# A decoder layer with two attention groups on one core: index evacuation, load order, projection order, last feed-forward block and closing work rearranged

## The chip, the cores and the metric

The kernel runs on one core of one Trainium2 chip. Its engines are TensorE (matrix products into PSUM), VectorE (DVE in the rows), ScalarE (ACT), GpSimd (POOL), and SyncE (SP), whose queue issues nearly all transfers. The metric is the device time of one execution in microseconds (us). All times of the rows are us from the first instruction of the program, unless marked ns.

## The reference, cut to what matters

One layer on 256 tokens of width 1024, all in 32-bit floats:

```python
a = rmsnorm(h, g_attn)
qa, ka, va, qi, ki, wi, qb, kb, vb = split(a @ w_in)   # rope on qa, ka, qi, ki, qb, kb; layernorm on ki first
score = sum_h w_h * relu(qi_h . ki)                     # token index: the top 64 earlier keys of each query
y_a = softmax(qa . ka over those keys) @ va             # 8 heads share one key/value head
y_b = softmax(qb . kb, causal) @ vb                     # 8 heads; one block of 256 keys here
h = h + concat(y_a, y_b) @ w_out
f = rmsnorm(h, g_ffn)
h = h + (silu(f @ w_gate) * (f @ w_up)) @ w_down        # inner width 2816
u = rmsnorm(h, g_ple)
h = h + sigmoid(u @ w_ple_gate) * (p @ w_ple_proj)
return rmsnorm(h, g_final)
```

## The kernel before, in words

**Products.** Every large product is made of three matmuls per tile, `mm3` (L169): each operand x is held as a rounded part H and a remainder L = x - H, and H.H, H.L and L.H are added up in PSUM. Activations are the stationary operand (128 by 128), weights the moving one (up to 512 columns). There are two token tiles, t = 0 and 1.

**Weights.** They come in chunks of mostly 1 MB in the order of `CHUNKS` (L40 to L52), one DMA each on SP's queue. `load` (L99) issues the DMA and has ScalarE round the chunk to `hi` in pieces of 1024 columns (L127); `split` (L131) has VectorE subtract to get `lo` (L154). `need` (L163) loads three chunks ahead and splits the one asked for. Most chunks rotate through three buffers each of `raw`, `hi` and `lo`, so a chunk's `hi` and `lo` can be written once TensorE is done with the chunk three before.

**Order.** TensorE's order is the order in which the code issues (L74). That of VectorE, ScalarE, GpSimd and SP is made by a scheduler, which takes the ready instruction of highest priority; priority is the order of issue, raised by `urgent`. Its order is fixed before the run and follows its own idea of times. From L774 on, the orders of TensorE, ScalarE and VectorE are those of the code.

**Start.** 36 small matmuls on zeros (`warm`, L206) run while the first data come. `load_a` (L212) brings x transposed and the first group of `w_in` columns, slice by slice. After these and the chunks of group 1, SP issues x by rows (`h`, L246), the table of cosines and sines (L248) and the gain of the index key (L250), and then `load(NS + 5)` the next three chunks (L257). ScalarE sums the squares of `h` (L256).

**Projections.** `piece` and `group` (L295, L311) multiply column group by column group: group 0 holds ka, va, qi, ki and wi, group 1 qb, 2 kb, 3 vb, 4 qa. The group's 8 slices run as 8 steps of six matmuls; after each, `tick` calls what the plan (L508 to L537) hangs there: transposes (`tp_idx`, `tp_rope`, `tp`), products of queries and keys (`qk_idx`, `qk`), products with the values (`pv`) and the top-64 search (`topk`). `evac_g0` (L333) takes group 0 out of PSUM: layernorm statistics, the norm of x by Newton steps on VectorE (`rsqrt`, L180), tables scaled by it for keys (`kcs`, VectorE) and queries (`qcs`, GpSimd, L349), then va, the index weights and the rotated index queries and keys (`r0`). `evac_rope` (L378) does the rotation of a later group.

**Attention.** Units B (all earlier keys) and A (selected keys) come as B[0], B[1], B[2], A[0], A[1], A[2]: the first of each is token tile 0 with all heads, the others tile 1 with four heads each. `qk` ends with the softmax: VectorE adds the mask and finds the least value (L454), ScalarE takes exponentials (L460), VectorE scales (L466). A's mask is `dmask`, which `topk` makes (L419). Ticks `pp` lie in the product p @ w_ple_proj, `wb` in the rows of w_out that belong to B (kk = 4 to 7), `wa` in those of A (kk = 0 to 3, tile 0).

**Feed-forward.** Six blocks of the inner width, five of 512 columns and one of 256. Each multiplies by w_gate for both tiles (j = 0), then by w_up (j = 1); `hid_T` (L662) transposes the product of a finished tile. Then come w_down (L710 on) and the gated embedding (`ple_mms`, `ple_evac`, L730 on).

**Close.** `ple_evac` (L740) applies the sigmoid, adds to `h`, sums squares (on ScalarE where no sum comes before it, otherwise on VectorE) and has GpSimd multiply by the last gain. Tile 1's second half runs as two blocks of 256 columns (L779). The two copies that scale tile 0 for the output (L785) are issued after the first of these. After the second come a square root (L788), a reciprocal and the last scaling: half the columns on VectorE with the gain (L791), half on ScalarE (L793), with one DMA each.

Of the kernel before, what the change touches and what calls it, by code (L numbers as in the profile page):

```python
# [16 lines left out]
P = 128  # L17
D = 1024
# [10 lines left out]
LOOK = 3  # L29
WARM = 36  # L30
NS = 2
# [8 lines left out]
def _chunks():  # L40

    out = []
    order = [(1, k, 1) for k in range(NS)] + [(1, k, 2) for k in range(NS, KD, 2)]
    order += [(g, k, 4) for g in range(2, 5) for k in (0, 4)]
    out += [(f"g{g}", k, nk, IN_GROUPS[g][1] - IN_GROUPS[g][0], "w_in", IN_GROUPS[g][0]) for g, k, nk in order]
    out.append(("pp", 0, 2, D, "w_ple_proj", 0))
    out += [("wo", k0, 2, D, "w_out", 0) for k0 in (4, 6, 0, 2)]
    for b, (f0, fw) in enumerate(FF_BLOCKS):
        out += [(f"f{b}_{j}", k0, 4, fw, w, f0) for j, w in enumerate(("w_gate", "w_up")) for k0 in (0, 4)]
# [9 lines left out]
def layer_kernel(  # L59
# [117 lines left out]
    def tsl(t):  # L177
        return slice(t * P, (t + 1) * P)
# [86 lines left out]
    with actx:  # L265
# [29 lines left out]
        def piece(g, pss, k, ts):  # L295

            if g == 0:
                (wH, wL), r = g0[k], slice(None)
            else:
                c0 = max(c[1] for c in chunks if c[0] == f"g{g}" and c[1] <= k)  # L300
                wH, wL = need(f"g{g}", c0)
                wH, wL = wH[:, k - c0, :], wL[:, k - c0, :]
            width = wH.shape[1]
            for n, (aT, wT) in enumerate(((XH, wH), (XL, wH), (XH, wL)) if len(ts) > 1 else ((XH, wH), (XH, wL), (XL, wH))):
# [68 lines left out]
        def tp_idx(t):  # L373
            transpose4(r0s[t].rearrange("p h d -> p (h d)"), idxT, t, f"tidx{t}")
# [127 lines left out]
        def at_tick(key, *fs):  # L502
            plan.setdefault(key, []).extend(fs)
# [169 lines left out]
    for b, (f0, w) in enumerate(FF_BLOCKS):  # L673
        pgu = {}
        for j in range(2):
            for t in range(NT):
                ps = acc(f"ff{b}{t}{j}")
                for k in range(KD):
                    wH, wL = need(f"f{b}_{j}", k - k % 4)
                    mm3(  # L680
                        ps[:, :w], FH[:, k, tsl(t)], FL[:, k, tsl(t)], wH[:, k % 4, :], wL[:, k % 4, :],
                        k == 0, k == KD - 1,
                    )
                    if (b, j, t) == (0, 0, 0) and k in (4, 7):
                        trn(1, int(k == 7), FH, FL, "f")
                pgu[(j, t)] = ps
                if b == 0 and (j, t) == (0, 0):
                    rf[1] = rstd_h(1, "f")
                if pend:
                    hid_T(*pend.pop(0))  # L690
                if j == 0:
                    sg = ff.tile([P, NQ], F32, tag="sg", name=f"sg{b}{t}", bufs=3)
                    nc.scalar.activation(sg[:, :w], ps[:, :w], AF.Silu, scale=rf[t])  # L693
                    pgu[("s", t)] = sg
                else:
                    hid = ff.tile([P, NQ], F32, tag="hid", name=f"hid{b}{t}", bufs=3)
                    nc.vector.scalar_tensor_tensor(  # L697
                        hid[:, :w], ps[:, :w], rf[t], pgu[("s", t)][:, :w], op0=ALU.mult, op1=ALU.mult
                    )
                    pend.append((b, t, hid, w))  # L700
# [8 lines left out]

    for k in range(TAILK):  # L710
# [28 lines left out]

    def ple_evac(t, f0, w, ps, prev):  # L740
        cc = slice(f0, f0 + w)
# [5 lines left out]
        s3 = sm.tile([P, 1], F32, tag="s3", name=f"s3{t}{f0}")  # L747
        if prev is None:
            nc.scalar.activation(sqt[:, :w], h[:, t, cc], AF.Square, accum_out=s3)
        else:  # L750
            nc.vector.tensor_tensor_reduce(
                sqt[:, :w], h[:, t, cc], h[:, t, cc], 1.0, prev, ALU.mult, ALU.add, s3
            )
# [20 lines left out]
    with tc.manual_schedule(engines={mybir.EngineType.PE, mybir.EngineType.Activation, mybir.EngineType.DVE}):  # L774
        sp = ple_evac(1, 0, NQ, ps, None)
        m = sm.tile([P, 1], F32, tag="m3", name="m30")
        nc.vector.tensor_scalar(m, s0, 1.0 / D, EPS, op0=ALU.mult, op1=ALU.add)
        r = rsqrt(m, 1, "o0")
        for j in range(2):  # L779
            ps = acc(f"pg11{j}")  # L780
            ple_mms(1, 1, ps, j * 256, 256)
            sp = ple_evac(1, NQ + j * 256, 256, ps, sp)
            if j == 0:
                for a in (0, NQ):
                    nc.scalar.activation(h[:, 0, a : a + NQ], h[:, 0, a : a + NQ], AF.Copy, scale=r)  # L785
                    nc.sync.dma_start(out[tsl(0), a : a + NQ], h[:, 0, a : a + NQ])
        rt = sm.tile([P, 1], F32, tag="m3", name="rt")
        nc.scalar.activation(rt, sp, AF.Sqrt, bias=eps, scale=1.0 / D)  # L788
        r = sm.tile([P, 1], F32, tag="m3r", name="r1")
        nc.vector.reciprocal(r, rt)  # L790
        nc.vector.scalar_tensor_tensor(h[:, 1, NQ:], h[:, 1, NQ:], r, gB["fin"][:, NQ:], op0=ALU.mult, op1=ALU.mult)  # L791
        nc.sync.dma_start(out[tsl(1), NQ:], h[:, 1, NQ:])
        nc.scalar.activation(h[:, 1, :NQ], h[:, 1, :NQ], AF.Copy, scale=r)  # L793
        nc.scalar.dma_start(out[tsl(1), :NQ], h[:, 1, :NQ])

# [15 lines left out]
def _pack(inputs):  # L811
# [4 lines left out]
    def rows(w):  # L816
# [42 lines left out]
```

## Time and profile before

| | |
|---|---|
| median of 3 runs | 339.21 us (339.17 to 339.3) |
| the profiled execution | 339.18 us |
| its span, first to last instruction | 337.4 us |
| granted TensorE clock, mean | 0.996 |
| TensorE busy | 326.0 us, 97% of the span |
| VectorE busy | 226.1 us, 67% |
| ScalarE busy | 175.4 us, 52% |
| moved by DMA | 59.71 MB, mean 177 GB/s |

A timeline row gives start, duration, engine, line, operation, output and inputs, shapes, the count of instructions merged into it, and in brackets the idle time of the engine before it and who ended it. Matmuls overlap in the rows (a row's duration is longer than the distance to the next start), so a matmul's cost is the distance of starts. PEld is the load of the stationary operand, which overlaps the matmul before it.

### The profile page before, as it was taken

How to read it: one execution, taken by the hardware profiler on the slowest of the kernel's cores; microseconds unless marked ns; L12 is line 12 of the kernel's file. 1: busy time of each engine (PE TensorE's matmuls, PEld its weight loads, DVE VectorE, ACT ScalarE, POOL GpSimd, SP SyncE). 2: the span in 40 equal slices, each digit the busy share in tenths (PEclk: the TensorE clock that was granted, in tenths of full speed). 3: DMA queues.
4: the chain of work that ended last, by engine and by line, in shares of the span. 5: the costliest groups of instructions: out<-in, count | busy, mean ns of one | idle time of the engine just before them, and what ended most of it. 6: DMA issues, size and time to landing. Idle time of an engine off the chain costs nothing.

```text
span 337.4 us, 4461 instructions
## 1 busy us (share of the span) xinstructions
PE 326.0 (97%) x1688; PEld 268.2 (79%) x1688; DVE 226.1 (67%) x459; ACT 175.4 (52%) x280; POOL 6.9 (2%) x17
## 2 busy tenths in 40 slices
PE   8999899998999999999999999999999999999991
PEld 8886777776777888888888888889988888888890
DVE  3969999999996695535644655344673535379854
ACT  4865366667785475533553454324643424238524
POOL 2000000000000000000000000000000000000130
PEclk9999999999999999999999999999999999999998
DMA  7995694301933056356436634344785555550003
GB/s 263 421 375 216 243 349 152 125 2 34 339 111 110 32 200 246 130 236 246 142 120 243 248 105 150 121 124 158 287 300 184 193 172 202 176 199 1 2 0 124
DMA packets 10677, 59.71 MB, mean 177 GB/s; under 512 B 1312, under 2 KB 1440, under 8 KB 4640
## 3 DMA queue, kind: packets, MB, share of 16 engines
q1 hardware_dynamic: 10512, 59.17, 48.8%
q8 instruction: 13, 0.21, 0.2%
q10 hardware_dynamic: 144, 0.26, 0.2%
q14 instruction: 8, 0.07, 0.1%
HBM read 58.38 MB, written 1.05 MB: 176 GB/s over the span
## 4 chain that ended last, share of the span: by engine, by line
PE 83%; DVE 10%; ACT 4%; issue 1%; ACTq 0%; DVEq 0%
PE ff L172 12%; PE ff L170 12%; PE ff L171 12%; PE g L306 9%; PE wd L171 6%; PE wd L170 6%; PE wd L172 6%; PE wo L170 2%; PE wo L172 2%; PE wo L171 2%; DVE lo L154 2%; PE pg L172 2%; PE pg L170 2%; PE pg L171 2%; PE hidt L666 1%; PE warm L206 1%
## 5 line engine op out<-in xcount | busy, mean ns | idle before, releaser
L154 DVE TENSOR_TENSOR lo<-raw,hi 128x1024 fp32r<-128x1024 f32 (+1 forms) x99 | 116.8, 1209 | 61.5 <-ACT hi L127 61.5
L127 ACT CAST hi<-raw 128x1024 fp32r<-128x1024 f32 (+1 forms) x99 | 99.0, 1040 | 95.8 <-PE ff L172 44.6
L170 PE MATMUL ff<-hi,FH 128*128 128x512 f32 (+1 forms) x192 | 72.4, 377 | 0.0
L172 PE MATMUL ff<-hi,FL 128*128 128x512 f32 (+1 forms) x192 | 71.4, 372 | 0.0
L171 PE MATMUL ff<-lo,FH 128*128 128x512 f32 (+1 forms) x192 | 71.3, 371 | 0.0
L172 PEld LDWEIGHTS ff<-hi,FL 128*128 128x128 f32 x192 | 36.1, 188 | 6.3
L171 PEld LDWEIGHTS ff<-lo,FH 128*128 128x128 f32 x192 | 36.2, 189 | 6.0
L170 PEld LDWEIGHTS ff<-hi,FH 128*128 128x128 f32 x192 | 36.2, 188 | 5.9
L170 PE MATMUL wd<-hi,hidH 128*128 128x512 f32 x88 | 35.1, 399 | 0.0
L171 PE MATMUL wd<-lo,hidH 128*128 128x512 f32 x88 | 35.0, 397 | 0.0
L172 PE MATMUL wd<-hi,hidL 128*128 128x512 f32 x88 | 34.5, 393 | 0.0
L306 PE MATMUL g<-hi,XH 128*128 128x512 f32 x64 | 25.9, 410 | 0.0
L306 PE MATMUL g<-hi,XL 128*128 128x512 f32 x64 | 24.9, 393 | 0.0
L306 PE MATMUL g<-lo,XH 128*128 128x512 f32 x56 | 21.8, 395 | 1.8 <-DVE lo L154 1.8
L170 PEld LDWEIGHTS wd<-hi,hidH 128*128 128x128 f32 x88 | 16.5, 188 | 4.0
L172 PEld LDWEIGHTS wd<-hi,hidL 128*128 128x128 f32 x88 | 16.5, 188 | 4.0
L171 PEld LDWEIGHTS wd<-lo,hidH 128*128 128x128 f32 x88 | 16.5, 188 | 3.7
L670 DVE TENSOR_TENSOR hidL<-hidt,hidH 128x512 fp32r<-128x512 f32 (+1 forms) x12 | 7.7, 644 | 12.8 <-ACT hidH L669 12.8
L697 DVE SCALAR_TENSOR_TENSOR hid<-ff,f_y,sg 128x512 f32<-128x512 f32 (+1 forms) x12 | 8.4, 704 | 11.5 <-PE ff L172 11.5
L693 ACT ACTIVATE sg<-ff,f_y 128x512 f32<-128x512 f32 (+1 forms) x12 | 7.8, 647 | 15.6 <-PE ff L172 15.6
L306 PEld LDWEIGHTS g<-hi,XH 128*128 128x128 f32 x64 | 12.1, 189 | 3.4 <-issue 1.0
L306 PEld LDWEIGHTS g<-lo,XH 128*128 128x128 f32 x56 | 10.5, 188 | 4.5 <-DVE lo L154 2.7
(199 smaller groups left out, 457.6 us busy)
## 6 DMA issues: line engine op xcount, KB each, us to landing
raw<-in_w_dram SPq DMA_DIRECT2D x46, 1024.0 KB, 4.9
a<-in_xa_dram SPq DMA_DIRECT2D x8, 354.5 KB, 6.7
raw<-in_w_dram SPq DMA_DIRECT2D x5, 512.0 KB, 3.6
raw_g<-in_w_dram SPq DMA_DIRECT2D x2, 512.0 KB, 8.0
h<-in_x_dram SPq DMA_DIRECT2D x1, 1024.0 KB, 9.9
out_dram<-h SPq DMA_DIRECT2D x3, 256.0 KB, 2.1
raw<-in_w_dram SPq DMA_DIRECT2D x2, 256.0 KB, 4.5
gBffn<-in_g_ffn_dram SPq DMA_DIRECT2D x1, 512.0 KB, 6.5
```

Of the source, the lines that this page charges most:

```text
L127: nc.scalar.copy(hi[:, o : o + step], raw[:, o : o + step])
L154: nc.vector.tensor_tensor(lo[:, o:e], raw[:, o:e], hi[:, o:e].bitcast(F32), op=ALU.subtract)
L170: nc.tensor.matmul(ps, aH, wH, start=start, stop=False)
L171: nc.tensor.matmul(ps, aH, wL, start=False, stop=False)
L172: nc.tensor.matmul(ps, aL, wH, start=False, stop=stop)
L206: nc.tensor.matmul(wps[:, :P], wz, wz, start=i == 0, stop=i == WARM - 1)
L306: nc.tensor.matmul(pss[t][:, :width], aT[:, k, tsl(t)], wT, start=k == 0 and n == 0, stop=k == KD - 1 and n == 2,)
L666: nc.tensor.transpose(pt[:, i * P : (i + 1) * P], hid[:, i * P : (i + 1) * P], ident)
L670: nc.vector.tensor_tensor(hidL[:, kk, tsl(t)], pv, hidH[:, kk, tsl(t)].bitcast(F32), op=ALU.subtract)
L693: nc.scalar.activation(sg[:, :w], ps[:, :w], AF.Silu, scale=rf[t])
L697: nc.vector.scalar_tensor_tensor(hid[:, :w], ps[:, :w], rf[t], pgu[("s", t)][:, :w], op0=ALU.mult, op1=ALU.mult)
```

## The change

- 33 matmuls in `warm` in place of 36; at slice 0 of groups 0 and 1 the product with the weights' remainder runs ahead of that with x's remainder.
- The chunk for slices 0 to 3 of group 2 is loaded ahead of `h`, the table and the index gain.
- `evac_g0` is cut in two: `norm_g0` (statistics, norms, `kcs`, `qcs`) stays; what takes va, the index weights and the rotated index queries and keys out of PSUM comes after group 1, its rotation and one more split of weights. `tp_idx` moves from ticks g3 0 and 1 to g3 4 and 5, `qk_idx` from g3 4 and 5 to g3 7 and g4 0; kb's transposes go to g4 0 and 1, B[0].qk to g4 2, B[1].pv to pp 3, B[2].pv to wb 1, and A[0].qk runs ahead of the last transpose of qa.
- The projection with w_out runs all four kk of tile 0 and then those of tile 1.
- The last feed-forward block has w_gate's and w_up's 256 columns side by side in one chunk and one operand of 512.
- w_down's first two rows of blocks run pair by pair of (t, c); the last `hid_T` moves from k = 4 to k = 6.
- Close: the norm of tile 0 and its two output copies come with the first half of tile 1; tile 1's first sum of squares and its products with the last gain go to VectorE; the last scaling is cut at column 384, with no gain in it.

```diff
-WARM = 36
+WARM = 33
...
+        if 2 * fw > NQ:
+            out += [(f"f{b}_{j}", k0, 4, fw, w, f0) for j, w in enumerate(("w_gate", "w_up")) for k0 in (0, 4)]
+        else:
+
+            out += [(f"f{b}_0", k0, 4, 2 * fw, ("w_gate", "w_up"), f0) for k0 in (0, 4)]
...
     split(NS + 2)
+    load(NS + 3)
     h = act.tile([P, NT, D], F32, tag="h", name="h")
     nc.sync.dma_start(h, x)
...
-        def evac_g0(pss):
+        def norm_g0(pss):
             mv = sm.tile([P, NT, 2], F32, tag="mv", name="mv", bufs=1)
...
+            state["sk"] = mv, sk
+
+        def evac_g0(pss):
+            rx, (mv, sk) = rxk["rx"], state["sk"]
+            for t in range(NT):
                 nc.scalar.activation(va[:, t, :], pss[t][:, 64:128], AF.Copy, scale=rx[:, t : t + 1])
...
-        at_tick(("g3", 0), lambda: tp_idx(0))
-        at_tick(("g3", 1), lambda: tp_idx(1))
...
-        at_tick(("g3", 4), lambda: qk_idx(0))
-        at_tick(("g3", 5), lambda: qk_idx(1))
-        at_tick(("g3", 7), lambda: tp_rope(2, 0, kbT))
-        at_tick(("g4", 0), lambda: tp_rope(2, 1, kbT))
-        at_tick(("g4", 1), B[0].qk)
+        at_tick(("g3", 4), lambda: tp_idx(0))
+        at_tick(("g3", 5), lambda: tp_idx(1))
+        at_tick(("g3", 7), lambda: qk_idx(0))
+        at_tick(("g4", 0), lambda: qk_idx(1), lambda: tp_rope(2, 0, kbT))
+        at_tick(("g4", 1), lambda: tp_rope(2, 1, kbT))
+        at_tick(("g4", 2), B[0].qk)
...
-        at_tick(("pp", 2), B[1].pv, tp(B[2], 0))
-        at_tick(("pp", 3), tp(B[2], 1), lambda: tp_rope(4, 0, qaT))
-        at_tick(("wb", 0), B[2].pv, lambda: tp_rope(4, 1, qaT))
-        at_tick(("wb", 0), A[0].qk)
+        at_tick(("pp", 2), tp(B[2], 0))
+        at_tick(("pp", 3), B[1].pv, tp(B[2], 1), lambda: tp_rope(4, 0, qaT))
+        at_tick(("wb", 0), A[0].qk, lambda: tp_rope(4, 1, qaT))
+        at_tick(("wb", 1), B[2].pv)
...
-        evac_g0(p0)
+        norm_g0(p0)
         split(NS + 4)
 
         group(1, p1, NS)
         rx = rxk["rx"]
         evac_rope(1, p1, qcs, "qb")
+        split(NS + 5)
+        evac_g0(p0)
...
-        for kk in (4, 5, 6, 7):
-            for t in range(NT):
+        for t in range(NT):
+            for kk in (4, 5, 6, 7):
                 for c in range(2):
                     wo_mms(kk, t, c)
-                tick("wb", 2 * (kk - 4) + t)
+                tick("wb", 4 * t + kk - 4)
...
+    for t, c in ((0, 0), (0, 1), (1, 0), (1, 1)):
+        for k in range(2):
+            wd_mms(k, t, c)
+    for k in range(2, TAILK):
...
-        if k == 4:
+        if k == 6:
             hid_T(*pend.pop(0))
...
-        if not (t == 1 and f0 >= NQ):
+        if mid:
+            mid()
+        if t == 0:
             nc.gpsimd.tensor_tensor(h[:, t, cc], h[:, t, cc], gB["fin"][:, cc], op=ALU.mult)
+        else:
+            nc.vector.tensor_tensor(h[:, t, cc], h[:, t, cc], gB["fin"][:, cc], op=ALU.mult)
...
+        def out0():
+            for a in (0, NQ):
+                nc.scalar.activation(h[:, 0, a : a + NQ], h[:, 0, a : a + NQ], AF.Copy, scale=r)
+                nc.sync.dma_start(out[tsl(0), a : a + NQ], h[:, 0, a : a + NQ])
+
+        sp = ple_evac(1, 0, NQ, ps, None, out0)
...
+        cut = 384
+        nc.vector.tensor_scalar(h[:, 1, cut:], h[:, 1, cut:], r, None, op0=ALU.mult)
+        nc.sync.dma_start(out[tsl(1), cut:], h[:, 1, cut:])
+        nc.scalar.activation(h[:, 1, :cut], h[:, 1, :cut], AF.Copy, scale=r)
+        nc.scalar.dma_start(out[tsl(1), :cut], h[:, 1, :cut])
```

## Rows read from the trace of the kernel before

**Rows 1.** Page, part 1: busy time, share of the span and instructions of each engine.

```profile
PE 326.0 (97%) x1688; PEld 268.2 (79%) x1688; DVE 226.1 (67%) x459; ACT 175.4 (52%) x280; POOL 6.9 (2%) x17
```

**Rows 2.** TensorE's own waits: us in total, times, longest us.

```profile
PE g L306 <- DVE lo L154: 1.8, 2, 1.5
...
PE pv_b L487 <- ACT pT_b L475: 1.0, 1, 1.0
```

**Rows 3.** Windows: stretch, busy time (instructions) by engine, clock, DMA share, GB/s.

```profile
18.00:26.00 8.00, 8.00 (x36) 6.51 (x36) 4.78 (x24) 5.20 (x10) 1.20 (x2) 1.00 0.92 383
...
65.00:75.00 10.00, 10.00 (x64) 7.72 (x63) 10.00 (x45) 6.82 (x21) 0.00 (x0) 1.00 0.01 2
```

**Rows 4.** Timeline of TensorE at the start of the run.

```profile
0.97 4.02 PE L206 MATMUL warm<-wz 128*128 128x128 bf16 x36 [0.97 <-DVE wz L203]
...
5.65 0.95 PE L306 MATMUL g<-ahi,XL 128*128 128x452 f32 x2
...
6.40 0.80 PE L306 MATMUL g<-alo,XH 128*128 128x452 f32 x2
```

**Rows 5.** Timeline of TensorE: the matmul behind the longest wait.

```profile
34.79 0.50 PE L306 MATMUL g<-lo,XH 128*128 128x512 f32 x1 [1.48 <-DVE lo L154]
```

**Rows 6.** Timeline of VectorE: wait for x, and the split that TensorE waits for.

```profile
21.96 0.17 DVE L339 TENSOR_SCALAR mm<-ssx 128x2 f32<-128x2 f32 x1 [1.80 <-ACT junk L256]
...
33.52 1.21 DVE L154 TENSOR_TENSOR lo<-raw,hi 128x1024 fp32r<-128x1024 f32 x1
```

**Rows 7.** Timeline of TensorE at the wait of B[1].pv.

```profile
79.59 1.09 PE L487 MATMUL pv_b<-pT_b,vb 128*64 128x128 f32 x14 [1.02 <-ACT pT_b L475]
```

**Rows 8.** Timeline: last softmax scaling of B[0] and A[0], and the transposes behind each.

```profile
67.60 0.69 DVE L466 TENSOR_TENSOR pr_b<-pr_b,rc_b 128x512 f32<-128x512 f32 x1
...
68.63 0.60 PE L473 MATMUL pt_b<-ident,pr_b 128*128 128x128 f32 x4
...
93.10 0.69 DVE L466 TENSOR_TENSOR pr_a<-pr_a,rc_a 128x512 f32<-128x512 f32 x1
...
94.88 0.60 PE L473 MATMUL pt_a<-ident,pr_a 128*128 128x128 f32 x4
```

**Rows 9.** Timeline of TensorE: 71 matmuls of 512 columns, then 71 of 256.

```profile
215.23 0.39 PE L171 MATMUL ff<-lo,FH 128*128 128x512 f32 x1
...
231.10 0.39 PE L172 MATMUL ff<-hi,FL 128*128 128x512 f32 x1
...
235.19 0.28 PE L171 MATMUL ff<-lo,FH 128*128 128x256 f32 x1
...
243.59 0.28 PE L172 MATMUL ff<-hi,FL 128*128 128x256 f32 x1
```

**Rows 10.** Timeline of the end.

```profile
329.29 1.33 ACT L785 ACTIVATE h<-h,o_y 128x512 f32<-128x512 f32 x2 [1.76 <-DVE o_y L194]
...
329.57 0.42 DVE L745 TENSOR_TENSOR h<-h,sgp 128x256 f32<-128x256 f32 x1
...
329.57 0.28 PE L172 MATMUL pg<-hi,UL 128*128 128x256 f32 x1
...
330.53 0.45 ACT L743 ACTIVATE sgp<-pg,u_y 128x256 f32<-128x256 f32 x1
...
332.46 0.30 ACT L788 ACTIVATE rt<-s,eps 128x1 f32<-128x1 f32 x1 [0.18 <-DVE s L751]
...
333.05 0.72 ACT L793 ACTIVATE h<-h,r 128x512 f32<-128x512 f32 x1 [0.29 <-DVE r L790]
```

**Rows 11.** Instructions on `score`: duration ns min/median/max, first and last start.

```profile
L419 DVE TENSOR_SCALAR dmask<-score x2: 215/252/289, 71.0 to 89.2; 128x128 f32<-128x128 f32 x1, 128x256 f32<-128x256 f32 x1
```

**Rows 12.** Timeline of GpSimd and VectorE: scaling of `qcs`; a small operation beside GpSimd.

```profile
24.80 1.26 POOL L349 TENSOR_SCALAR qcs<-cst_cs,rq 128x128 f32<-128x128 f32 x2 [22.41 <-DVE rq L344]
...
327.24 1.29 POOL L755 TENSOR_TENSOR h<-h,gBfin 128x512 f32<-128x512 f32 x1 [4.09 <-ACT sq_o L749]
...
327.33 1.22 DVE L190 SCALAR_TENSOR_TENSOR o_a<-o_y,o_h 128x1 f32<-128x1 f32 x1
```

More of the change, by code (lines that the diff above doesn't have):

```diff
@@ L48, in _chunks @@
     for b, (f0, fw) in enumerate(FF_BLOCKS):
-        out += [(f"f{b}_{j}", k0, 4, fw, w, f0) for j, w in enumerate(("w_gate", "w_up")) for k0 in (0, 4)]
+        if 2 * fw > NQ:
+            out += [(f"f{b}_{j}", k0, 4, fw, w, f0) for j, w in enumerate(("w_gate", "w_up")) for k0 in (0, 4)]
+        else:
+            out += [(f"f{b}_0", k0, 4, 2 * fw, ("w_gate", "w_up"), f0) for k0 in (0, 4)]
     out += [("wd", k0, 2, D, "w_down", 0) for k0 in range(0, KF, 2)]
@@ L303, in piece @@
             width = wH.shape[1]
-            for n, (aT, wT) in enumerate(((XH, wH), (XL, wH), (XH, wL)) if len(ts) > 1 else ((XH, wH), (XH, wL), (XL, wH))):
+            for n, (aT, wT) in enumerate(((XH, wH), (XL, wH), (XH, wL)) if len(ts) > 1 and k else ((XH, wH), (XH, wL), (XL, wH))):
                 for t in ts:
@@ L674, in layer_kernel @@
         pgu = {}
-        for j in range(2):
+        both = 2 * w <= NQ
+        cw = 2 * w if both else w
+        for j in range(1 if both else 2):
             for t in range(NT):
@@ L680, in layer_kernel @@
                     mm3(
-                        ps[:, :w], FH[:, k, tsl(t)], FL[:, k, tsl(t)], wH[:, k % 4, :], wL[:, k % 4, :],
+                        ps[:, :cw], FH[:, k, tsl(t)], FL[:, k, tsl(t)], wH[:, k % 4, :], wL[:, k % 4, :],
                         k == 0, k == KD - 1,
@@ L694, in layer_kernel @@
                     pgu[("s", t)] = sg
-                else:
+                if j == 1 or both:
+                    up = ps[:, cw - w : cw]
                     hid = ff.tile([P, NQ], F32, tag="hid", name=f"hid{b}{t}", bufs=3)
                     nc.vector.scalar_tensor_tensor(
-                        hid[:, :w], ps[:, :w], rf[t], pgu[("s", t)][:, :w], op0=ALU.mult, op1=ALU.mult
+                        hid[:, :w], up, rf[t], pgu[("s", t)][:, :w], op0=ALU.mult, op1=ALU.mult
                     )
@@ L708, in wd_mms @@
         mm3(pd[(t, c)], hidH[:, k, tsl(t)], hidL[:, k, tsl(t)], wH[:, k % 2, cc], wL[:, k % 2, cc], k == 0, k == KF - 1)
-    for k in range(TAILK):
+    for t, c in ((0, 0), (0, 1), (1, 0), (1, 1)):
+        for k in range(2):
+            wd_mms(k, t, c)
+    for k in range(2, TAILK):
         for t in range(NT):
@@ L738, in ple_mms, with ple_evac @@
                 hook(k)
-    def ple_evac(t, f0, w, ps, prev):
+    def ple_evac(t, f0, w, ps, prev, mid=None):
         cc = slice(f0, f0 + w)
@@ L747, in ple_evac @@
         s3 = sm.tile([P, 1], F32, tag="s3", name=f"s3{t}{f0}")
-        if prev is None:
+        if prev is None and t == 0:
             nc.scalar.activation(sqt[:, :w], h[:, t, cc], AF.Square, accum_out=s3)
@@ L751, in ple_evac @@
             nc.vector.tensor_tensor_reduce(
-                sqt[:, :w], h[:, t, cc], h[:, t, cc], 1.0, prev, ALU.mult, ALU.add, s3
+                sqt[:, :w], h[:, t, cc], h[:, t, cc], 1.0, 0.0 if prev is None else prev, ALU.mult, ALU.add, s3
             )
-        if not (t == 1 and f0 >= NQ):
+        if mid:
+            mid()
+        if t == 0:
             nc.gpsimd.tensor_tensor(h[:, t, cc], h[:, t, cc], gB["fin"][:, cc], op=ALU.mult)
+        else:
+            nc.vector.tensor_tensor(h[:, t, cc], h[:, t, cc], gB["fin"][:, cc], op=ALU.mult)
         return s3
@@ L774, in layer_kernel @@
     with tc.manual_schedule(engines={mybir.EngineType.PE, mybir.EngineType.Activation, mybir.EngineType.DVE}):
-        sp = ple_evac(1, 0, NQ, ps, None)
         m = sm.tile([P, 1], F32, tag="m3", name="m30")
@@ L778, in layer_kernel @@
         r = rsqrt(m, 1, "o0")
+        def out0():
[3 more added lines that the diff above has]
+        sp = ple_evac(1, 0, NQ, ps, None, out0)
+        rt = sm.tile([P, 1], F32, tag="m3", name="rt")
+        sums = [sp]
         for j in range(2):
@@ L781, in layer_kernel @@
             ple_mms(1, 1, ps, j * 256, 256)
[L782 to L788, printed above, removed]
+            sums.append(ple_evac(1, NQ + j * 256, 256, ps, sums[-1]))
+        nc.scalar.activation(rt, sums[-1], AF.Sqrt, bias=eps, scale=1.0 / D)
         r = sm.tile([P, 1], F32, tag="m3r", name="r1")
         nc.vector.reciprocal(r, rt)
[L791 to L794, printed above, removed]
+        cut = 384
[3 more added lines that the diff above has]
+        nc.scalar.dma_start(out[tsl(1), :cut], h[:, 1, :cut])
 _INS = ["xa", "x", "pT", "w", "g_k", "g_ffn", "g_ple", "g_fin", "cs"]
@@ L821, in _pack, with cols @@
     w0 = a["w_in"][0][:, IN_GROUPS[0][0] : IN_GROUPS[0][1]].reshape(KD, P, W0)
-    flat = [
-        rows(a[name][0][k0 * P : (k0 + nk) * P, c0 : c0 + width]).ravel() for _, k0, nk, width, name, c0 in CHUNKS
-    ]
+    def cols(names, r0, r1, c0, width):
+        names = names if isinstance(names, tuple) else (names,)
+        n = width // len(names)
+        return np.concatenate([a[name][0][r0:r1, c0 : c0 + n] for name in names], axis=1)
+    flat = [rows(cols(name, k0 * P, (k0 + nk) * P, c0, width)).ravel() for _, k0, nk, width, name, c0 in CHUNKS]
     return {
```

## The prediction, written before the result

> **What bounds the kernel now.** I read the page's busy times first: TensorE is busy for 326.0 of 337.4 us, so only TensorE's idle time, its matmul count and the two ends can give anything [rows 1]. Next TensorE's own waits: two waits for a split of weights on VectorE, 1.8 us together, and one wait of 1.0 us for a transposed softmax in B[1].pv [rows 2]. They lie between 26 and 80 us. The windows of that part show why: VectorE is busy for all of 10 us from 65 to 75 [rows 3]. So there two engines are nearly full at once; what TensorE is freed from early it keeps only if VectorE delivers the later operands earlier too. From the feed-forward on TensorE waits for nobody, and a matmul there costs its distance of starts. Last the end: after the last matmul's end at 329.57 + 0.28 = 329.85 a chain over ScalarE, VectorE and two transfers fills the rest [rows 10].
>
> **The sum** is made against the profiled execution, 339.18 us, which is 0.03 under the median of the runs; its span is 337.4, and I leave the 1.78 around it as they are.
>
> **Fewer warm matmuls.** 36 run from 0.97 to about 4.75, 0.105 each [rows 4]; three fewer let the first product start 0.32 earlier, if its operands are there. That time is still at the lower clock: two matmuls of 452 columns take 6.40 - 5.65 = 0.75, 0.375 each [rows 4], which is 1.2 GHz, while later 512 columns take 0.227 [rows 9], so 452 would take 0.20. Work begun 0.32 earlier at that pace saves 0.32 x 0.20 / 0.375 = 0.17. Bounds: 0.32 if the rise to 2.4 GHz comes that much earlier as well, 0 if operands are late. The swap of remainders at slice 0 moves no matmul in or out.
>
> **The chunk ahead of x.** On SP's queue x, the cosine table and the index gain now stand behind one more 1 MB chunk. At 383 GB/s [rows 3] that is 1.05 / 0.383 = 2.7 us: the squares on ScalarE, the norm on VectorE, `kcs`, and `qcs` on GpSimd start 2.7 later. VectorE now idles 1.80 for x [rows 6]; that becomes some 4.5, in which it can split the early chunk, 2 x 1.21 = 2.4 [rows 6]. So VectorE is about even afterwards (0.3 behind), with the norm late and the split early. The rotation of group 1 waits for the norm, but its transposes stand at g3 2, far behind; I take nothing.
>
> **Index evacuation behind group 1.** The matmul at 34.79 had waited 1.48 for a split that VectorE began at 33.52, in the middle of the index evacuation [rows 5, 6]. With the norm alone in front, and both splits of group 2 ahead of the evacuation, this wait and its smaller companion go: 1.8 [rows 2]. Each restart also costs about 0.1, which I leave for the range. What is late next: the index queries and scores, by three ticks, each of six matmuls of 0.227, so 3 x 1.36 = 4.1; behind them stand the top-64 searches, which now end at 71.0 (tile 0) and 89.2 (tile 1) [rows 11]. On GpSimd nothing is queued behind `qcs`.
>
> **B[1].pv one tick later.** The idle 1.02 [rows 7] goes, since six matmuls and four transposes now lie between the copy and its use. Behind it B[2].pv and A[0].qk shift on TensorE without loss, unless A[0]'s chain is late.
>
> **What VectorE takes back.** TensorE is then 2.0 ahead at B[0]'s second transposes and 3.0 ahead at A[0]'s. Before, B[0]'s operand was ready at 67.60 + 0.69 = 68.29 for a start at 68.63, a slack of 0.34; A[0]'s at 93.79 for 94.88, a slack of 1.09 [rows 8]. If VectorE kept its times, 2.0 - 0.34 = 1.66 would return at B[0], and of the remaining 1.34 another 0.25 at A[0]: 1.9 in all. Nothing returns if B[0]'s scaling passes the scores and search rounds, which are now later in the order of issue. B[0].qk itself stands one tick later, nearer to its transposes. Between 0 and 1.9 I take 0.7, under the middle, because the searches that shared VectorE with B[0] are later.
>
> **Projection by token tile.** The same 96 matmuls. The first chunk of w_out is held two ticks longer, so rounding and splitting of the chunk that takes its buffers come later; they lie beside the tile-1 half. If that cover were gone, it would be one split piece, 1.21 [rows 6]. Taken at 0.
>
> **Last feed-forward block.** 96 matmuls of 256 columns become 48 of 512. A 256-column one costs (243.59 - 235.19) / 70 = 0.120, a 512-column one (231.10 - 215.23) / 70 = 0.2267 [rows 9]. 96 x 0.120 - 48 x 0.2267 = 11.52 - 10.88 = 0.64. Bytes, rounding and splitting stay the same. The two accumulators of the block are now freed by a sigmoid-linear unit and a product; w_down's new pair order gives them 18 matmuls, 4.1 us, which covers both. Nothing else is on the path.
>
> **Close.** The last sigmoid started at 330.53, although its product ended at 329.85, because ScalarE was at the two output copies of tile 0 (1.33 from 329.29) [rows 10]. They now go out three microseconds earlier: gain 0.68. The product with the last gain, 0.42 for 256 columns, now lies on VectorE between the sum and the reciprocal, beside the square root of 0.30: cost 0.1 [rows 10]. At the very end ScalarE scales 384 columns in place of 512, 0.72 less a quarter of the width; from 0.45 for 256 columns the slope is 0.27 per 256, so 0.59 and a gain of 0.13 [rows 10]. VectorE's 640 columns take 0.289 + 3 x 0.074 = 0.51 by the searches' mask rows (0.215 for 128, 0.289 for 256) [rows 11], less than ScalarE. The two last transfers carry the same bytes. Together 0.7, bounds 0.3 to 0.9.
>
> **Sum:** 0.17 + 1.8 + 1.0 - 0.7 + 0.64 + 0.7 = 3.6; 339.18 - 3.6 = 335.6 us. Without loss on VectorE it is 334.9; with every term at its better bound (0.15 more at the start, 0.2 for restarts, 0.2 at the close) 334.3.
>
> **Rivals.**
>
> *VectorE gives all of it back.* The order of VectorE is made by a scheduler, so the code's new order need not remove the waits, only move them; that would be the change not doing what it says. For it: VectorE is full from 26 us on [rows 3] and its work is unchanged. Against it: the split's lateness is a matter of order, not of amount. Then only start, block and close remain: 339.18 - 0.17 - 0.64 - 0.7 = 337.7. Chance 0.17.
>
> *GpSimd holds VectorE up.* A one-column operation of VectorE took 1.22 while GpSimd multiplied from 327.24 to 328.53, and ended with it [rows 12]. `qcs` takes 1.26 on GpSimd [rows 12]; before, it ran while VectorE had little to do, now the splits of group 2 are due there. If VectorE loses that time and, being full, passes it on, 335.6 + 1.26 = 336.8. Against it: those splits have some 2 us to spare. Chance 0.08. The Trainium skill, page "SBUF — State Buffer", section "SBUF: two separate sides", says that an operation with two SBUF inputs and one of GpSimd take a shared pair of ports exclusively, the later one being blocked in full. By that rule this is the time to expect; the row of 1.22 agrees with it.
>
> *Slower: A[0] comes late.* Its transposes would be due at 94.88 - 3.0 = 91.9. If its scaled softmax, ready at 93.79 before [rows 8], is put off by x (2.7) and by the three ticks of the index branch (4.1) together, it is ready at 100.6, a stall of 8.7: 339.18 - 4.3 + 8.7 = 343.6. It turns slower once that operand is later than before by over 3.1. With x's 2.7 alone the stall is 4.6 and the time 339.5, no change. Against it: tile 0's search needs to be done only by then, and it ended at 71.0, some 20 us ahead [rows 11]. Chances 0.07 and 0.05.
>
> **How the numbers follow.** The forecast has 0.63. I count as no change what lies within 0.2%, 0.68 us, about what a measurement of this kernel can tell. Faster: 0.63 + 0.17 + 0.08 = 0.88; same 0.05; slower 0.07. The range goes from the sum of better bounds, 334.3, to just above the first rival, 337.9; outside lie the 0.12 of the last two cases and little else.
>
> **What would show it.** Right: no TensorE wait for `lo` between 26 and 36 us; B[1].pv without idle time; no 256-column matmul in `ff`, 48 more of 512 and 96 fewer in all of that block; last sigmoid within 0.1 of the last matmul's end; last matmul near 326.8. Wrong: new TensorE waits at `pt_b`, `pt_a` or `tr`, for VectorE or ScalarE, of over 2 us together; a late rise of the granted clock; or a wait for a `lo` of w_out.

## The result, and the profile after

The changed kernel takes **340.97 us** in the median of 12 runs (340.12 to 342.88), against 339.22 us before: ratio 1.0056, 95% interval 1.004 to 1.0072. It is slower by 1.75 us, where 335.6 us, a gain of 3.6, was forecast. The profiled execution is the longest of the twelve, 342.88 us with a span of 341.0; its mean granted clock is 0.984, and over the twelve runs that mean goes from 0.983 to 0.996, the last in the run of 340.12. So the profile shows 1.9 us more of loss than the median run has; the other eleven left no trace. Three runs far above the others of their kernel (410 and 466 us in experiments 2 and 5, 659 us of the kernel before) count in no median, range or ratio here.

The start of TensorE's first matmul of each part, from the timelines of before, after, and of the first experiment below:

| us | before | after | split put first |
|---|---|---|---|
| first product | 4.75 | 4.43 | 4.39 |
| group 2 | 26.83 | 26.45 | 25.55 |
| group 3 | 40.14 | 37.35 | 36.45 |
| group 4 | 55.44 | 57.30 | 49.98 |
| p @ w_ple_proj | 72.83 | 78.37 | 70.05 |
| w_out | 83.28 | 87.32 | 79.00 |
| feed-forward | 117.88 | 122.78 | 115.36 |
| w_down | 243.85 | 248.18 | 240.76 |
| gated embedding | 306.62 | 311.12 | 303.70 |
| last matmul | 329.57 | 334.08 | 326.66 |
| end of span | 337.39 | 341.01 | 333.59 |

Up to group 3 the change was 2.8 us ahead, where 2.0 was forecast. Between there and p @ w_ple_proj it lost 8.3 us. TensorE's own waits, in total, times and longest, in place of the 1.8 and 1.0 of [rows 2]:

```profile
PE g L311 <- DVE lo L158: 3.4, 1, 3.4
...
PE pt_b L483 <- DVE pr_b L476: 1.8, 1, 1.8
```

The first of them in TensorE's timeline of the changed kernel (start, duration, engine, line, operation):

```profile
43.62 0.48 PE L311 MATMUL g<-hi,XH 128*128 128x512 f32 x1
47.51 0.79 PE L311 MATMUL g<-lo,XH 128*128 128x512 f32 x1 [3.41 <-DVE lo L158]
48.10 0.63 PE L311 MATMUL g<-hi,XL 128*128 128x512 f32 x1
48.53 0.63 PE L311 MATMUL g<-hi,XH 128*128 128x512 f32 x1
...
54.26 0.39 PE L311 MATMUL g<-hi,XL 128*128 128x512 f32 x1
54.49 0.39 PE L311 MATMUL g<-hi,XH 128*128 128x512 f32 x1
```

At this place, behind a transpose, the matmul with `lo` should start 0.32 after 43.62 (one step earlier the two starts are 41.79 and 42.11) and starts 3.89 after: 3.57 lost. Then come matmuls 0.43 apart (48.10 to 48.53) where they are 0.23 apart later (54.26 to 54.49). The windows of the changed kernel say why; the columns are stretch, busy time and instructions of TensorE, its weight loads, VectorE, ScalarE and GpSimd, granted clock, DMA share, GB/s:

```profile
30.00:43.60 13.60, 13.60 (x66) 11.25 (x65) 13.60 (x36) 6.71 (x9) 0.00 (x0) 1.00 0.70 253
43.60:47.50 3.90, 0.50 (x4) 0.19 (x2) 3.90 (x10) 2.34 (x3) 0.00 (x0) 0.89 0.00 0
47.50:53.50 6.00, 5.99 (x17) 4.72 (x18) 6.00 (x6) 0.59 (x1) 0.00 (x0) 0.50 0.56 194
53.50:58.00 4.50, 4.50 (x27) 3.51 (x26) 1.00 (x3) 2.52 (x4) 0.00 (x0) 1.00 1.00 371
```

While TensorE waited, its clock fell from 2.4 to 1.2 GHz, and the 6 us after the wait ran at half speed. From the matmul at 47.51 to the first of slice 6, at 53.71, it takes 6.20; in experiment 1, at full clock, the same instructions take 3.34 (43.05 to 46.39): another 2.9 lost. With the 1.8 at B[0]'s transposes that is 3.6 + 2.9 + 1.8 = 8.3, what the table shows. These are the longest run's; as the mean clocks differ, the part of the clock is not the same in every run.

What VectorE did instead of that split, in its timeline, and below it ScalarE's rounding of the same chunk:

```profile
42.55 0.68 DVE L325 TENSOR_TENSOR kb<-g,kcs 128x512 f32<-128x512 f32 x1
43.15 0.54 DVE L332 TENSOR_TENSOR r0b<-r0b,r_t 128x384 f32<-128x384 f32 x1
43.62 0.41 DVE L326 TENSOR_TENSOR kb_t<-g,kcs 128x256 f32<-128x256 f32 x1
...
44.38 0.68 DVE L325 TENSOR_TENSOR kb<-g,kcs 128x512 f32<-128x512 f32 x1
...
45.91 0.41 DVE L329 TENSOR_TENSOR kb_t<-g,kcs 128x256 f32<-128x256 f32 x1
46.24 1.21 DVE L158 TENSOR_TENSOR lo<-raw,hi 128x1024 fp32r<-128x1024 f32 x1
```

```profile
32.10 2.01 ACT L131 CAST hi<-raw 128x1024 fp32r<-128x1024 f32 x2 [0.65 <-PE g L311]
```

The chunk was rounded by 34.1 us. (Which chunk a rounding belongs to follows from the three buffers: this one takes the buffer of group 2's first chunk, which TensorE left at about 32; the next rounding, at 37.55, waits for the end of group 2 and is group 4's.) From 37.6 to 44.1 VectorE took out the index part (rows `r0b`, `kn`, `ki_t`, `r_t`), from 42.55 on mixed with the rotation of kb, and only at 46.24 it began the split that TensorE had been waiting for since 43.9.

Of what was forecast to be seen: there is no wait for a split between 26 and 36 us, B[1].pv has no idle time, the last block has no matmul of 256 columns. Of the signs of being wrong one came, waits at `pt_b` and `pt_a` of 1.8 + 0.4 = 2.2 us; a wait for a split of group 3, which cost most, was not among them. The close is as forecast, against [rows 10]; the last sigmoid starts 0.04 after the last matmul's end:

```profile
334.08 0.28 PE L176 MATMUL pg<-hi,UL 128*128 128x256 f32 x1
```

```profile
334.40 0.47 ACT L761 ACTIVATE sgp<-pg,u_y 128x256 f32<-128x256 f32 x1 [2.36 <-PE pg L176]
...
336.35 0.29 ACT L814 ACTIVATE rt<-s,eps 128x1 f32<-128x1 f32 x1 [0.18 <-DVE s L769]
336.35 0.42 DVE L777 TENSOR_TENSOR h<-h,gBfin 128x256 f32<-128x256 f32 x1
336.70 0.15 DVE L816 RECIPROCAL r<-rt 128x1 f32<-128x1 f32 x1
336.88 0.61 ACT L820 ACTIVATE h<-h,r 128x384 f32<-128x384 f32 x1 [0.24 <-DVE r L816]
```

From the last matmul's start to the end it takes 341.01 - 334.08 = 6.93 us, before 7.82.

### The profile page after: what moved, and what is told of

Its sections match the earlier page's. It is cut to its first block, busy times and chain, and to the rows that moved or that the text cites. A ratio compares the mean times of both kernels' runs of the same rounds, so it can differ in the third digit from the quotient of the medians.

```text
span 341.0 us, 4346 instructions
## 1 busy us (share of the span) xinstructions
PE 327.8 (96%) x1637; PEld 266.8 (78%) x1637; DVE 227.7 (67%) x464; ACT 174.3 (51%) x278; POOL 5.6 (2%) x16
## 4 chain that ended last, share of the span: by engine, by line
PE 76%; DVE 11%; ACT 2%; issue 1%; ACTq 0%; DVEq 0%
PE ff L174 12%; PE ff L176 12%; PE ff L175 12%; PE wd L174 6%; PE wd L175 6%; PE wd L176 6%; PE g L311 3%; DVE lo L158 3%; PE pg L176 2%; PE pg L174 2%; PE pg L175 2%; PE wo L174 2%; PE wo L176 2%; PE wo L175 2%; PE hidt L677 1%; ACT hi L131 1%
## 5 line engine op out<-in xcount | busy, mean ns | idle before, releaser
L174 PE MATMUL ff<-hi,FH 128*128 128x512 f32 x176 | 69.6, 396 | 0.0
L176 PE MATMUL ff<-hi,FL 128*128 128x512 f32 x176 | 68.6, 390 | 0.0
L175 PE MATMUL ff<-lo,FH 128*128 128x512 f32 x176 | 68.5, 389 | 0.0
L176 PEld LDWEIGHTS ff<-hi,FL 128*128 128x128 f32 x176 | 33.0, 188 | 7.1
L175 PEld LDWEIGHTS ff<-lo,FH 128*128 128x128 f32 x176 | 33.1, 188 | 6.4
L174 PEld LDWEIGHTS ff<-hi,FH 128*128 128x128 f32 x176 | 33.1, 188 | 6.4
L311 PE MATMUL g<-lo,XH 128*128 128x512 f32 x56 | 22.7, 411 | 3.4 <-DVE lo L158 3.4
L311 PE MATMUL g<-hi,XL 128*128 128x512 f32 x64 | 25.8, 408 | 0.0
```

The costliest lines, as they stand in the source:

```text
L174: nc.tensor.matmul(ps, aH, wH, start=start, stop=False)
L175: nc.tensor.matmul(ps, aH, wL, start=False, stop=False)
L176: nc.tensor.matmul(ps, aL, wH, start=False, stop=stop)
L311: nc.tensor.matmul(pss[t][:, :width], aT[:, k, tsl(t)], wT, start=k == 0 and n == 0, stop=k == KD - 1 and n == 2,)
```

## The experiments

Each kernel was timed beside the kernel before, whose median was 339.07 to 339.25 in these sessions.

**1. The split put first.** To the changed kernel:

```diff
         group(2, p2)
+        split(NS + 6)
         evac_rope(2, p2, kcs, "kb")
```

> The changed kernel, with the split of the second chunk of group 3 issued ahead of the rotation of kb (one line). The same work, x as late as in the changed kernel. Theory (order): TensorE stood still for 3.4 us because VectorE rotated kb, eight operations, before a split whose rounded part had been there since 38.6 us; then this wait shrinks to under 1 us, the granted clock does not fall around 46 us, and 3.4 + 3.0 us are won, less what the units of group B give back: 334 to 337.5 us. Rival (amount): VectorE, put 3.8 us behind by the later x, has too much to do in any order; then a wait of 2 us or more stands at this or the next split, and the time stays at 339 us or above.

Measured 335.56 us, ratio 0.9885 (0.9869 to 0.9902). VectorE's timeline of this kernel:

```profile
41.54 1.22 DVE L158 TENSOR_TENSOR lo<-raw,hi 128x1024 fp32r<-128x1024 f32 x1
42.68 0.55 DVE L332 TENSOR_TENSOR r0b<-r0b,r_t 128x384 f32<-128x384 f32 x1
43.14 1.22 DVE L158 TENSOR_TENSOR lo<-raw,hi 128x1024 fp32r<-128x1024 f32 x1
44.28 0.19 DVE L373 COPY r0b<-r0b 128x64 f32<-128x64 f32 x1
44.38 0.68 DVE L325 TENSOR_TENSOR kb<-g,kcs 128x512 f32<-128x512 f32 x1
```

and its windows over the same stretch as above:

```profile
43.60:47.50 3.90, 3.90 (x23) 3.23 (x22) 3.90 (x9) 2.53 (x5) 0.00 (x0) 1.00 0.56 166
47.50:53.50 6.00, 5.87 (x36) 4.18 (x35) 5.91 (x8) 3.92 (x6) 0.00 (x0) 1.00 0.52 173
```

One line takes 5.4 us off. VectorE is as busy as before (3.90 of 3.90) and TensorE does not wait: the fault was order, not amount, and the later x did not cause it. The index part still runs ahead of the split here; what no longer does is the rotation of kb. (The 38.6 us of the expectation belongs to group 4's chunk; the right one, in the changed kernel, was rounded by 34.1, so the split could have been done earlier still.) What is left of TensorE's waits:

```profile
PE pt_a L483 <- DVE pr_a L476: 1.0, 2, 0.8
...
PE pt_b L483 <- ACT pr_b L470: 0.6, 1, 0.6
```

The two at `pt_a` are A[0]'s, 0.76 at 91.56, and A[2]'s, 0.29 at 104.49; two expectations below take the second for A[1]'s.

**2. The wait filled.** To the changed kernel, behind the first matmul of slice 4 in group 3:

```diff
+                if (g, k, n) == (3, 4, 0) and 0 in ts:
+                    fill = aux("fill")
+                    for _ in range(26):
+                        nc.tensor.matmul(fill[:, :256], XH[:, 0, tsl(0)], XH[:, 1, :], start=True, stop=True)
```

> The changed kernel with 26 matmuls of 256 columns, whose product nobody reads, put on TensorE just ahead of the matmul that waits 3.4 us for the split of group 3 (26 x 0.12 = 3.1 us). The wait itself is not shortened. Theory: the granted clock fell at 46.7 us because TensorE had nothing to do from 44.1 us on; then it does not fall here, the six microseconds after the wait run at 0.227 per 512 columns instead of 0.427, and the time falls by some 2.5 to 3 us, to 338 to 339. Rival: the clock falls for another reason (the load of the chip, chance); then it falls here as well, in some runs at least, and the time stays at 340.5 to 341.5.

Measured 338.53 us, ratio 0.9976 (0.9967 to 0.9986), with a mean clock of 0.993 to 0.995. VectorE's order is that of the changed kernel until the index scores, and differs a little behind. TensorE's timeline and the window behind it:

```profile
43.10 0.48 PE L311 MATMUL g<-hi,XH 128*128 128x512 f32 x1
43.41 3.27 PE L318 MATMUL fill<-XH 128*128 128x256 f32 x26
46.52 0.50 PE L311 MATMUL g<-lo,XH 128*128 128x512 f32 x1
```

```profile
47.50:53.50 6.00, 6.00 (x36) 4.72 (x35) 5.85 (x6) 2.35 (x4) 0.00 (x0) 1.00 0.72 259
```

The needed work is held up for 3.42 us (43.10 to 46.52), nearly as long as the 3.89 of the changed kernel, but the clock stays up, and 2.4 us of the median come back. The fall is a consequence of TensorE's standing still. Not all of the 2.4 is the clock's: the hold-up is 0.5 shorter, and the wait at B[0] shrinks from 1.8 to 1.2:

```profile
PE pt_b L487 <- ACT pr_b L474: 1.2, 1, 1.2
```

That leaves, as an estimate, 1.3 for the clock in the median run, against 2.9 in the profiled one.

**3. x early.** The changed kernel without its `load(NS + 3)` ahead of `h`.

> The changed kernel, but x, the table and the index gain go out ahead of the first chunk of group 2, as before. Theory (order): the norm comes 3 to 4 us earlier; the scheduler may then place the splits otherwise, and if the wait of 3.4 us goes the time is 334 to 337.5, as with the split put first. Rival (the later x is the cause): the same 334 to 337.5 here, but no gain from putting the split first. If the wait stays although x is early, neither holds alone and the time is 339 or above.

Measured 336.64 us, ratio 0.9917 (0.9902 to 0.9931). The scheduler, given an earlier norm, itself puts the first half of the split ahead of kb's rotation (41.05 against 42.95), so the long wait is gone here too; by experiment 1 the later x is not what made it. There is another wait, in TensorE's timeline:

```profile
27.43 0.50 PE L310 MATMUL g<-lo,XH 128*128 128x512 f32 x1 [1.15 <-DVE lo L158]
```

With x early VectorE is at the norm when the first chunk of group 2 comes, and its split is late by 1.15. So the later x, which brings this chunk sooner, is worth about 336.64 - 335.56 = 1.1 us, where the forecast had put it at nothing.

**4. The index evacuation early.** The changed kernel with

```diff
         norm_g0(p0)
+        evac_g0(p0)
...
         split(NS + 5)
-        evac_g0(p0)
```

> The changed kernel, but the index evacuation is issued right behind the norms again, ahead of group 1's last steps and of the two splits; x late, and all else as changed. Theory (order on VectorE): what is issued ahead of a split delays it. Here the index evacuation, some 7 us of VectorE's work that starts about 31 us, stands between the two halves of the second chunk of group 2, so TensorE waits 2 to 4 us for the second half near 37 us, while the splits of group 3 come ahead of the rotation of kb and the wait of 3.4 us goes. If the wait is over 3 us the clock may fall too: 337 to 341 us. Rival (the move of the index evacuation is itself the fault): putting it back gives the full gain, 334 to 336 us.

Measured 339.28 us, ratio 1.0005 (0.9995 to 1.0016). TensorE's waits:

```profile
PE g L311 <- DVE lo L158: 2.1, 2, 1.2
PE pt_b L483 <- DVE pr_b L476: 1.8, 1, 1.8
```

Two waits of about 1 us for splits of groups 2 and 3 instead of one of 2 to 4, but the sum and the place (behind the index evacuation) are the theory's. The rival falls: moving the index evacuation is right, 339.28 - 335.56 = 3.7 us better, once the split behind it is seen to.

**5. The two ends alone.** The kernel before with `WARM = 33`, the swap at slice 0, the last block, w_down's order and the close of the change.

> The kernel before with only the two ends of the change: 33 warm matmuls and the swap at slice 0, the last feed-forward block in one operand with the new order of w_down's first rows, and the close. Load order, index evacuation, ticks and projection order as before; the orders of VectorE and ScalarE up to the feed-forward are those of the kernel before. Theory: these parts are worth what the landmarks of the two traces say, 0.4 at the start, 0.6 in the block, 0.9 at the close, less 0.2 in w_down: 337.2 to 337.9 us. Rival (the clock, or VectorE in the middle, takes the start back): 337.9 to 338.4. If the parts themselves cost time: 339.2 or above.

Measured 338.12 us, ratio 0.9958 (0.9941 to 0.9974): 1.1 us, in the rival's range. Its profiled execution took 337.29, 1.9 better than the kernel before's, with every landmark within 0.2 of where the theory put it; the other runs took 0.5 to 1 us more, and as none of them left a profile, where that lies stays open.

**6. B[1].pv early.** Experiment 1 with

```diff
-        at_tick(("pp", 2), tp(B[2], 0))
-        at_tick(("pp", 3), B[1].pv, tp(B[2], 1), lambda: tp_rope(4, 0, qaT))
+        at_tick(("pp", 2), B[1].pv, tp(B[2], 0))
+        at_tick(("pp", 3), tp(B[2], 1), lambda: tp_rope(4, 0, qaT))
```

> The changed kernel with the split put first, and B[1].pv back at its old tick, one earlier. Theory: the wait of 1.0 us for the transposed softmax comes back, as in the kernel before: 336.2 to 336.8 us against 335.6 with the late tick. Rival (later waits take back whatever is won here): 335.4 to 335.9, as the waits for A[0] and A[1], 1.0 us in all, shrink by what this one costs.

Measured 335.48 us, ratio 0.9887 (0.987 to 0.9904). The rival's time, not its reason: the wait of [rows 7] simply does not return. ScalarE had copied the transposed softmax by 74.74, and the product starts at 75.15. What took the wait away was the rest of the new order; the tick is worth nothing here.

**7. 36 warm matmuls.** Experiment 1 with `WARM = 36` and the old order at slice 0.

> The changed kernel with the split put first, and 36 warm matmuls and the old order at slice 0. Theory: the start is worth about 0.2, so 335.8. Rival (the moment at which the granted clock rises differs from run to run by more, 4.1 to 6.9 us in the profiles so far, and the operands limit the first products): no difference, 335.4 to 335.7.

Measured 335.76 us (335.49 to 335.89), ratio 0.9895 (0.9879 to 0.991), against 335.47 to 335.99: not to be told apart.

**8. The projection as before.** Experiment 1 with `for kk` outside and `for t` inside, and the ticks numbered accordingly.

> The changed kernel with the split put first, and the projection in its old order, both tiles of one row of w_out after each other. Theory (from the forecast, which put this part at nothing): 335.4 to 335.8. Rival: by token tile the second chunk of w_out is due two ticks earlier and the first is held longer; if one of these cost or gave time, a wait for a split of w_out appears or goes, and the time moves by over 0.4 us either way.

Measured 335.14 us (335.0 to 335.24), ratio 0.9879 (0.9866 to 0.9892). The projection by token tile costs 0.4: these four runs lie below the four of experiment 1 (335.47 to 335.99), though the intervals of the two ratios overlap. Not at a split: the rival's place was wrong too. Of 0.37 between the two profiles in this part 0.31 lies at A[1]'s product with the values. ScalarE in experiment 1, and then here:

```profile
99.58 1.04 ACT L131 CAST hi<-raw 128x1024 fp32r<-128x1024 f32 x1
100.52 0.58 ACT L485 COPY pT_a<-pt_a 128x512 f32<-128x512 f32 x1
```

```profile
99.20 1.04 ACT L131 CAST hi<-raw 128x1024 fp32r<-128x1024 f32 x1
100.14 0.58 ACT L485 COPY pT_a<-pt_a 128x512 f32<-128x512 f32 x1
```

The product starts at 100.83 and 100.84, and needs the second copy half-way: from its start to the next instruction's it takes 1.34 where the copy ends at 101.10, and 1.03 where it ends at 100.72. The rounding of a weight chunk stands in front of that copy in both, 0.38 later in experiment 1; why it comes later there was not followed up.

**9 to 11. The waits that are left.** Three tries on them: experiment 1 with B[0]'s transposes and product one tick later; experiment 1 with the softmax of B[0] raised in priority; the same with A[0]'s raised too.

```diff
-        at_tick(("g4", 5), tp(B[0], 0))
-        at_tick(("g4", 6), tp(B[0], 1))
-        at_tick(("g4", 6), B[2].qk)
-        at_tick(("g4", 7), B[0].pv, lambda: topk(0))
+        at_tick(("g4", 6), tp(B[0], 0), B[2].qk)
+        at_tick(("g4", 7), tp(B[0], 1))
+        at_tick(("g4", 7), lambda: topk(0))
+        at_tick(("pp", 0), B[0].pv)
```

> The changed kernel with the split put first, and the transposes of B[0] and its product with the values one tick later. Theory: the wait of 0.6 us for B[0]'s softmax and its restart go, and nothing else depends on them: 334.8 to 335.2 us. Rival (what is won is waited for at A[0] and A[1], whose operands are VectorE's last): 335.4 to 335.8.

```diff
+        def uq(u):
+            def f():
+                with urgent():
+                    u.qk()
+            return f
...
-        at_tick(("g4", 2), B[0].qk)
+        at_tick(("g4", 2), uq(B[0]))
```

> The changed kernel with the split put first, and the softmax of B[0] (mask, exponentials, scaling) raised in the scheduler's priority; the ticks stay. VectorE then takes B[0]'s scaling ahead of seven search instructions, and ScalarE's two roundings of weights no longer stand between its exponentials. Theory (order again): the wait of 0.6 us at B[0]'s transposes and its restart of 0.2 go, and as the searches are put off by under 2 us the later units stay as they are: 334.6 to 335.1 us. Rival (VectorE's work up to A[0] is what counts): the gain is waited for at A[0] and A[1] instead, 335.4 to 335.8.

```diff
-        at_tick(("wb", 0), A[0].qk, lambda: tp_rope(4, 1, qaT))
+        at_tick(("wb", 0), uq(A[0]), lambda: tp_rope(4, 1, qaT))
```

> As the kernel before this one, with A[0]'s softmax raised as well: it goes ahead of four instructions of tile 1's search. Theory (order): the wait of 0.8 us at A[0]'s second transposes goes too, 333.8 to 334.4 us. Rival (amount): tile 1's search and the split of w_out, which are put behind A[0], are late next, at A[1] or at a matmul of w_out, and the time is 334.6 us or above.

Measured 336.70 us, ratio 0.9925 (0.9909 to 0.9941); 335.66, 0.9897 (0.9882 to 0.9911); 338.33, 0.9967 (0.9955 to 0.9978). TensorE's waits with B[0] later:

```profile
PE wo L175 <- DVE lo L158: 1.5, 1, 1.5
...
PE pv_b L497 <- ACT pT_b L485: 0.6, 1, 0.6
```

with B[0] raised:

```profile
PE pt_a L483 <- DVE pr_a L476: 1.4, 2, 1.1
```

and with A[0] raised too:

```profile
PE pt_a L483 <- ACT pr_a L470: 1.9, 1, 1.9
...
PE qk_a L451 <- DVE mn_a L464: 0.9, 1, 0.9
```

Each try took the wait it aimed at away, and another came or grew: with B[0] later at a split of w_out, with B[0] raised at A[0]'s scaling (0.76 became 1.08), with A[0] raised too at A[2]'s scores, behind VectorE's pass over A[1]'s, and at A[1]'s exponentials. So the rivals are right for the two raised kernels; with B[0] later both ranges were too low and the place was another. In the last of them the clock fell again. Its windows:

```profile
92.90:99.20 6.30, 3.45 (x17) 2.08 (x17) 6.16 (x20) 3.90 (x12) 0.00 (x0) 1.00 0.48 159
99.20:102.60 3.40, 3.40 (x13) 2.71 (x12) 1.94 (x7) 1.90 (x6) 0.00 (x0) 0.50 0.60 251
```

Over its ten runs the mean clock goes with the time: 0.997 in the four of 337.13 to 337.67 us, 0.988 to 0.993 in the six of 338.26 to 338.86; the profiled run, 338.26, is one of these, so that the clock fell in the other five and not in the four is read from the means alone.

**12. A[0] later.** Experiment 8 with

```diff
-        at_tick(("wb", 4), tp(A[0], 1))
-        at_tick(("wb", 5), A[0].pv, A[2].qk)
-        at_tick(("wb", 6), tp(A[1], 0))
+        at_tick(("wb", 5), tp(A[0], 1), A[2].qk)
+        at_tick(("wb", 6), A[0].pv, tp(A[1], 0))
```

> The changed kernel with the split put first and the projection in its old order, and A[0]'s second transposes and its product with the values one tick later. Theory (only the tick is too early): the wait of 0.8 us at A[0]'s second transposes and its restart go, and A[1] and A[2], whose ticks stay, are no later: 334.2 to 334.6 us against 335.1. Rival (VectorE's order behind it decides, as when B[0] was put off): the later product puts off the scaling of A[1] or A[2], whose waits grow by as much: 335.0 us or above.

Measured 334.95 us (334.88 to 335.62), ratio 0.9883 (0.9867 to 0.99): not to be told from experiment 8, and between the two ranges. All waits for A's softmax went, and one for A[0]'s result came:

```profile
PE wo L176 <- DVE yL L505: 0.6, 1, 0.6
```

Experiments 8 and 12 beat both kernels, the one before by 4 us and the changed one by 6.

## Why the prediction was wrong

**The step that failed** is "Index evacuation behind group 1", and in it the sentence on what is late next. It followed the moved work to those who use it (index queries, scores, searches) and did not ask what stands behind it on VectorE. That is the split of group 3's second chunk. With the index part later, VectorE was still at it when kb was ready, and the rotation of kb, which is issued ahead of that split, came ahead of it too. The rotation is what made the split late: in experiment 1 the index part alone stands ahead of it, and there is no wait. The waits of 1.8 did go; one that cost 3.6 came, 13 us after the longer of them.

**The price of a wait** was wrong as well. I counted a wait at its length. This one cost, in the profiled run, its length, 2.9 more at half clock, and most of B[0]'s 1.8 behind it. The last is not the clock's in the main: where the wait was filled, 1.2 of it remained, where it was gone, 0.6.

**The rivals.** "VectorE gives all of it back" named the mechanism, that the scheduler's order need not remove waits, only move them; its price was bounded by what had been won, and the result lies 3.3 us above it. The rival on the slower side, A[0] late, did not happen: its transposes did not wait. GpSimd did not slow a split beside `qcs`: its last row ends at 28.62 + 1.26 = 29.88 and the next split begins at 29.94. VectorE only waited 0.43 for the first of the two tables, ahead of its rotation at 29.33. At the close the two did meet, in VectorE's and GpSimd's timelines of the changed kernel:

```profile
326.95 0.72 DVE L194 SCALAR_TENSOR_TENSOR o_a<-o_y,o_h 128x1 f32<-128x1 f32 x1
...
327.90 0.22 DVE L194 SCALAR_TENSOR_TENSOR o_a<-o_y,o_h 128x1 f32<-128x1 f32 x1
```

```profile
326.37 1.28 POOL L775 TENSOR_TENSOR h<-h,gBfin 128x512 f32<-128x512 f32 x1 [2.15 <-DVE s L769]
```

The first ends at 327.67, with GpSimd (327.65), and takes 0.72 where the next of its kind takes 0.22. This agrees with the rule of the Trainium skill, page "SBUF — State Buffer", section "SBUF: two separate sides", that the later of two such operations is blocked, which was weighed in the forecast; here it is off the path.

**The terms**, as far as the runs tell them apart:

- Start: the first product came 0.32 earlier, and group 2 by 0.4 and 1.3 in the two profiles of the table, whose clock rose at different times. With 36 of them, in experiment 7, it came at 4.28, earlier than with 33: the time of one was not the 0.105 that I took in every run. Experiment 7 cannot tell the three matmuls from nothing, and the 1.1 of experiment 5 is less than the block and the close alone; what the start is worth stays open.
- Index evacuation: group 2 took 2.4 less, not 1.8. The restarts, which I had left for the range at 0.1 each, cost more: from 32.92 to 35.12 in the kernel before, two distances of 0.227 and the wait of 1.48 leave 0.27.
- The chunk ahead of x: the norm came 25.77 - 21.96 = 3.8 later, not 2.7, and the part is worth 1.1, not nothing. In the forecast that gain stood under the index evacuation, which alone leaves a wait of 1.15 (experiment 3).
- B[1].pv: the 1.0 was won, but not by the tick (experiment 6).
- What VectorE takes back: 0.7 forecast; with the split first 0.6 + 1.0 of waits are left, near the upper end of the 0 to 1.9; 0.3 of it is at A[2], which I had not counted.
- Projection: nothing forecast, 0.4 lost (experiment 8).
- Last block: from the feed-forward's start to w_down's 125.97 before and 125.40 after, 0.57 for the 0.64 forecast. Of it w_down gave 0.17 back (62.77 and 62.94 to the gated embedding), which I had not priced.
- Close: 7.82 - 6.93 = 0.89 for 0.7. The product with the last gain cost none of its 0.1: it runs beside the square root from 336.35 on.

Experiment 1's 335.56 is the number forecast, and partly by chance. From before to experiment 1 the table gives, against the forecast: up to group 2 1.3 won (0.17), in group 2 2.4 (1.8), from group 3 to w_out 0.6 and from w_out to the feed-forward -1.8 (together +0.3), from there to the last matmul 0.4 (0.64), at the close 0.9 (0.7). What the units of attention and the projection lost more, the start and the restarts after waits gave.

## What to carry to other kernels

Where work is moved on an engine that is full, list what it is moved ahead of, on that engine and up to the next idle time, and ask of each item when its user needs it; who uses the moved work is only half of the question. A term for a wait on TensorE needs a second price: behind one of 3.4 us here the matmuls of 6 us ran at half the clock, and behind one of 1.5 us they did not. And where a scheduler makes the order, read its order after each edit: one issue moved by one line was worth 5.4 us here, and small raises of priority cost up to 2.8.

## What the runs showed of the hardware

The granted clock fell in the middle of a kernel whose TensorE is 96% busy. In the changed kernel it fell to half during one gap of 3.41 us; in the profiled run of experiment 11 it fell behind two gaps of 0.91 and 1.94, with 2.7 us of matmuls between them. The gap of 1.48 in [rows 5] left it up (1.00 over 30.0 to 43.6 us in the kernel before), and so did those of 0.90 and 1.18 in experiment 4 (1.00 over 33 to 47 us). The changed kernel's twelve runs go from 340.12 us (mean clock 0.996) to 342.88 (0.984), those of the kernel before beside them from 338.81 to 339.78; experiment 1's four go from 335.47 to 335.99. That the fall makes the spread is likely, not shown, as only one of the twelve left a trace; and the kernel before, which has no such gap, spread by 1.9 us in another session (338.75 to 340.68).
